# Last stage of a hybrid encoder block: the gated embedding is added to the residual by adding transfers, its squares are queued further back, and two column pairs take another order of units

## The chip, the cores and the metric

The kernel runs on one core of a Trainium2 chip. The metric is the device time of one execution in microseconds (us); the kernel before took 2026.38 us in the median of three runs (2024.7 to 2027.43).

## The reference

One layer on 256 rows of width 4096 in float32: an input product of 4096 by 14336, attention heads beside a convolution module, an output product that gives the residual `h`, and then the last stage, where the change lies:

```python
gate = jax.nn.sigmoid(rms_norm(h, ple_norm_g[i]) @ w_ple_gate[i] + b_ple_gate[i])
h = h + gate * (p[i] @ w_ple[i])
...
return rms_norm(h, final_g)
```

`w_ple_gate` is 4096 by 4096, `p[i]` is 256 by 256 and `w_ple` 256 by 4096.

## The kernel before, in words

**Products.** Every weight is split into a high part `wh` (a cast on ScalarE, ACT in the profile, L204) and a low part `wl` (weight minus high part, on VectorE, DVE, L205), and so is every operand. A product is then three matmuls of 128 by 512: high by high, low by high, high by low. Weights come in tiles `wt` of 128 rows by 1024 columns: two column blocks of 512 side by side. There are five buffers for `wt`, three each for `wh` and `wl`, two each for the sums `u`, `uh` and `ul` (the pools of L73 and L1085).

**Units.** `mixed_product` (L377) computes one pair of column blocks for both halves of the rows, in 16 units of two row blocks of weights each. A plain unit makes eight products (24 matmuls). A unit marked with a star in the order makes seven (21 matmuls), after Strassen: DVE builds the sums `ua` and `ub` of weight tiles (L518, L519, L531, L532), ACT and DVE split them as they split weights, and some products go to four helper banks (P1, P5, P6, P7) in place of the four accumulators. Its operands on the other side are combinations of row blocks made beforehand (`hS`, or the spare places that `combine_into_places`, L370, fills for pair 13). A minus in the order lets a transfer that adds, issued on GpSimd's queue (POOL), make the low part of the second weight tile: ACT writes the cast and its negative `low` (L215, L217), and the transfer adds the weight to `low`.

**Orders.** The stars stand in tables of numbers. `dense` has eight starred units, `denser` has nine, three of its units with a minus:

```python
dense = units("1 0* 3 2* 5 4* 6* 7 8* 9 10* 11 12* 14* 13 15")
denser = units("1 0* 3 2* 5 4* 13* 7- 6*- 8* 10*- 9 12* 14* 11 15")
```

**The last stage.** There are eight column blocks, so four pairs, `c0` = 0, 2, 4 and 6. The first three are made by `gated_pair` (L1236), with the orders `late`, `dense`, `dense`; the fourth has its own code from L1280 on with the order `final`. After its 16 units a pair makes the embedding `p @ w_ple` by `product` (L243), 24 matmuls into the banks `ps_tmp` that the helpers also use: there are four, and the embedding holds all of them until DVE has multiplied each by its gate. The gate of a quarter (row half h, column block j) is made by L1266 and a sigmoid on ACT (L1267). What then follows waits in the list `later`, of which `fill` takes four entries at the end of each unit of the next pair: the multiply of gate and embedding into `gt` (a half of a tile `z`), the add of `gt` to the residual `hc`, the sum of squares of `hc` (on ACT, L610) and the multiply of `hc` by the final weights (`fgs`). Entries of `later` all run under L184.

**What sets the order.** Each engine runs its instructions in one fixed order. The program's order is the wish; a scheduler fixes the queue of each engine when the kernel is built, and may move an instruction forward past others. The bias rows `rows` and the final weights `fgs` share three buffers with the rows that combinations are made in, so a load of one waits on its queue (SP) until another is done with.

Of the kernel before, what the change touches and what calls it, by code (L numbers as in the profile page):

```python
# [13 lines left out]
ALU = mybir.AluOpType  # L14
# [3 lines left out]
NB = 512  # L18
# [7 lines left out]
def hybrid_block(  # L26
# [23 lines left out]
    nc = tc.nc  # L50
# [129 lines left out]
    later = deque()  # L180
# [62 lines left out]
    def product(w, col, lhs, kblocks, pool=None, tag="acc", fills=2):  # L243

        acc = [
            (pool or ps_acc).tile([P, NB], F32, tag=tag, name=f"acc{h}") for h in range(NH)
        ]
        for k0 in range(0, kblocks, KC):
            kc = min(KC, kblocks - k0)
            wh, wl = weight_parts(w, col, k0, kc)  # L250
            for k in range(kc):
                for h in range(NH):
                    accumulate(acc[h], h, lhs, k0 + k, wh, wl, k, kblocks)
            fill(fills)
        return acc
# [10 lines left out]
    def sum_rows():  # L266
        return [spool.tile([P, NB], F32, tag="row", name="comb", bufs=3) for _ in range(2)]
# [33 lines left out]
    def combine_again(dst, at, t, i, rows, then=lambda ins: None, at_places=None):  # L301

        a, s = rows
        then(
            nc.vector.tensor_tensor(
                a.rearrange("q (i t) -> q i t", t=T), t[:, i : i + 2, 0, :].bitcast(F32),
                t[:, i : i + 2, 1, :].bitcast(F32), ALU.add,
            )
        )
        return combined_parts(  # L310
            dst, at, s, a[:, :T], a[:, T : T + P], a[:, T + P :], 1.0, then, at_places
        )
# [27 lines left out]
    def units(text):  # L340

        return [
            (int(u.rstrip("*+-")), "".join(f for f in "*+" if f in u), "-" in u)
            for u in text.split()
        ]


    dense = units("1 0* 3 2* 5 4* 6* 7 8* 9 10* 11 12* 14* 13 15")
    denser = units("1 0* 3 2* 5 4* 13* 7- 6*- 8* 10*- 9 12* 14* 11 15")
# [12 lines left out]
    late = units("1 3 5 7 9 11 13 15 0* 2 4* 6 8* 10* 12 14")  # L362

    def spare_places(tiles):

        return [[t[:, 0, q, P:] for q in range(2)] for t in tiles]
# [3 lines left out]
    def combine_into_places(pair, tiles):  # L370

        rows = sum_rows()
        places[pair] = spare_places(tiles[:4])
        t, i = tiles[pair // 2], pair % 2 * 2
        combine_again(None, None, t, i, rows, at_places=places[pair])()

    def mixed_product(  # L377
# [93 lines left out]
        for n, (pair, seven, by_dma) in enumerate(order):  # L471
# [82 lines left out]
            if begins and on_begin:  # L554
                on_begin()
# [13 lines left out]
    tt, stt = nc.vector.tensor_tensor, nc.vector.scalar_tensor_tensor  # L569
    QUARTERS = ((0, 0), (1, 0), (0, 1), (1, 1))  # L570

    def helper_sums(helper, z):


        nc.scalar.copy(z[1][0], helper["P1"])
        tt(z[1][0], helper["P6"], z[1][0], ALU.add)
        tt(z[0][1], helper["P5"], z[1][0], ALU.add)
        tt(z[1][0], helper["P7"], z[1][0], ALU.add)
        tt(z[1][1], helper["P5"], z[1][0], ALU.add)

    def sum_tiles(*homes):

        homes = homes or (dict(tag="stage"),) * 2
        t = [spool.tile([P, NH, NB], F32, name="z", **kw) for kw in homes]
        return t, [[t[j][:, h] for j in range(2)] for h in range(NH)]
# [57 lines left out]
    def first_pairs(add):  # L643
# [62 lines left out]
        for n in range(1, n_x + 1):  # L706
# [26 lines left out]
    rows = [(conv_ln_g, KCW), (conv_ln_b, KCW), (b_dw, KCW), (attn_out_g, AW // P),  # L733
            (conv_out_g, KCW), (ple_norm_g, KD)]
# [332 lines left out]
    def broadcast_row(src, n0, n, **kw):  # L1067

        kw = kw or dict(tag="row", bufs=3)
        t = spool.tile([P, n], F32, name="row", **kw)  # L1070
        nc.sync.dma_start(
            t, bass.AP(tensor=src.tensor, offset=src.offset + n0, ap=[[0, P], [1, n]])
        )
        return t
# [13 lines left out]
    for c0, order in zip(range(0, CW // NB, 2), point):  # L1088
        row = broadcast_row(b_pw, c0 * NB, 2 * NB, tag="stage")
        rows = [row[:, j * NB : (j + 1) * NB] for j in range(2)]  # L1090
# [85 lines left out]
    hs, hT, hS = [], [], []  # L1176
# [20 lines left out]
    for c0 in range(0, D // NB, 2):  # L1197
        for j in range(2):
            hc = act.tile([P, NH, NB], F32, tag="act", name="hc")
            c = c0 + j  # L1200
# [19 lines left out]
        for h, j in QUARTERS:  # L1220
            hc = hs[c0 + j][:, h, :]
# [10 lines left out]
    ssq_f = cpool.tile([P, NH, n_f + 2], F32, name="ssq_f")  # L1232
    nc.vector.memset(ssq_f[:, :, :1], EPS)
    square_f = partial(square_sum, scale=D ** -0.5)

    def gated_pair(c0, order, ahead):  # L1236

        z, rows, fgs = [], [], []

        def on_begin():  # L1240
            rows.extend(broadcast_row(b_ple_gate, (c0 + j) * NB, NB) for j in range(2))

        def on_helpers(helper):
            z.extend(sum_tiles()[1])
            stt(z[0][0], helper["P1"], r_h[:, :1], rows[0], ALU.mult, ALU.add)
            helper_sums(helper, z)
            for h, j in QUARTERS[1:]:
                zz = z[h][j]
                stt(
                    zz, zz, r_h[:, h : h + 1], rows[j],  # L1250
                    ALU.mult, ALU.subtract if j else ALU.add,
                )
            fgs.extend(broadcast_row(final_g, (c0 + j) * NB, NB) for j in range(2))

        acc = mixed_product(
            w_ple_gate[0], c0 * NB, hT, hS, order, on_helpers, ahead=ahead, fills=(4,),
            on_begin=on_begin,
        )
        pacc = [
            product(w_ple[0], (c0 + j) * NB, pT, PLE // P, pool=ps_tmp, tag="tmp", fills=0)  # L1260
            for j in range(2)
        ]
        todo = []
        for h, j in QUARTERS:
            gt, hc = z[h][j], hs[c0 + j][:, h, :]
            stt(gt, acc[h][j], r_h[:, h : h + 1], gt, ALU.mult, ALU.subtract if j else ALU.add)  # L1266
            nc.scalar.activation(gt, gt, AF.Sigmoid)  # L1267
            later.append(partial(tt, gt, pacc[j][h], gt, ALU.mult))
            todo.append(partial(tt, hc, hc, gt, ALU.add))
            todo.append(partial(square_f, ssq_f[:, h, 1 + c0 + j : 2 + c0 + j], hc))  # L1270
            todo.append(partial(tt, hc, hc, fgs[j], ALU.mult))
        later.extend(todo)

    for c0 in range(0, n_f - 2, 2):
        gated_pair(c0, dense if c0 else late, None if c0 else h_ahead)


    c0 = n_f - 2
# [9 lines left out]
    rows, fgs = [], []  # L1288

    def on_begin():  # L1290
        rows.extend(broadcast_row(b_ple_gate, (c0 + j) * NB, NB) for j in range(2))

    def scaled(h, j):
        zz = z[h][j]
# [2 lines left out]
    def on_helpers(helper):  # L1297
# [3 lines left out]

    acc, add_left = mixed_product(
        w_ple_gate[0], c0 * NB, hT, hS, final, on_helpers, fills=(4,), on_begin=on_begin,
        left=[None] * 3 + [kept] * 3,
    )
# [73 lines left out]
    squares = []  # L1379
# [45 lines left out]
```

## Time and profile before

| | |
|---|---|
| median of three runs | 2026.38 us |
| the profiled execution's own time | 2025.85 us |
| span of its profile | 2024.1 us |
| granted clock of TensorE over the span | 0.998 |
| `c0` = 2, from 1739.57 to 1826.60 us | 87.03 us |
| `c0` = 4, from 1826.60 to 1914.50 us | 87.90 us |

A stretch here goes from the start of the last matmuls of one pair (where L1266 begins) to the same place of the next. PE is TensorE's matmuls, PEld its weight loads, SP the queue that issues most transfers. The busy time of an engine counts overlapping instructions once; the mean duration of a DVE instruction is some 0.08 us longer than the distance to the next when they stand back to back.

### The profile page before, as it was taken

The numbers are of one execution on the slowest core, as the hardware profiler recorded it, in microseconds if no ns is written. First come the engines' busy times: TensorE is split into PE (matmuls) and PEld (weight loads), VectorE is DVE, ScalarE is ACT, GpSimd is POOL, SyncE is SP. The second block draws the span as 40 slices with busy tenths as digits, with TensorE's granted clock in tenths as the row PEclk, the third lists the DMA queues.
The fourth block names the chain that finished last, engine by engine and source line by source line (L and its number), as shares of the span: only waits on it lengthen the run. The fifth ranks groups of instructions, "written<-read, shape, count | busy, mean of one in ns | idle before, by whom it ended". The sixth has DMA issues, their size and how long they took to land.

```text
span 2024.1 us, 26329 instructions
## 1 busy us (share of the span) xinstructions
PE 2006.7 (99%) x9043; PEld 1648.0 (81%) x9043; DVE 1926.9 (95%) x2771; ACT 1257.1 (62%) x1634; POOL 65.3 (3%) x71
## 2 busy tenths in 40 slices
PE   9999999999999999999999999999999999999997
PEld 7888888878888888788888888887888888888876
DVE  7999999899999999888999999999999999999998
ACT  7655555665666556776566676765766766656565
POOL 0000000000000000000000000000000000000000
PEclk9999999999999999999999999999999999999999
DMA  8788878679668877556677786876767766666765
GB/s 290 225 233 241 249 221 250 178 220 257 200 198 257 255 206 235 164 176 205 202 239 215 225 244 209 240 239 204 236 215 230 234 200 200 211 218 206 232 207 180
DMA packets 174193, 447.72 MB, mean 221 GB/s; under 512 B 14302, under 2 KB 17518, under 8 KB 174058
## 3 DMA queue, kind: packets, MB, share of 16 engines
q1 hardware_dynamic: 161952, 417.93, 63.8%
q0 software_dynamic: 11456, 27.27, 7.9%
q8 instruction: 71, 1.16, 0.2%
q10 hardware_dynamic: 650, 0.84, 0.1%
q14 instruction: 64, 0.52, 0.1%
HBM read 441.78 MB, written 4.19 MB: 220 GB/s over the span
## 4 chain that ended last, share of the span: by engine, by line
PE 89%; DVE 6%; issue 2%; DMA 1%; ACT 1%; POOLq 0%; POOL 0%; ACTq 0%; DVEq 0%; SPq 0%
PE acc L420 68%; PE acc_P L420 17%; DVE wl L205 2%; DMA wt<-in_w_in_dram 1%; PE tmp_ps L170 1%; DVE cv L787 1%; PE acc L237 1%; DVE ul L205 1%; PE tmp_ps L959 0%; PE tmp_ps L943 0%; PE tmp_ps L977 0%; ACT uh L204 0%; DVE cv L868 0%; ACT wh L204 0%; PE tmp_ps L982 0%
## 5 line engine op out<-in xcount | busy, mean ns | idle before, releaser
L420 PE MATMUL acc<-wh,big_t 128*128 128x512 f32 x4028 | 1240.3, 391 | 0.9 <-ACT big_t L156 0.4
L204 ACT CAST wh<-wt 128x1024 fp32r<-128x1024 f32 (+1 forms) x716 | 684.3, 965 | 493.8 <-PE acc L420 351.7
L420 PEld LDWEIGHTS acc<-wh,big_t 128*128 128x128 f32 x4028 | 753.3, 188 | 157.1 <-issue 1.3
L205 DVE TENSOR_TENSOR wl<-wt,wh 128x1024 fp32r<-128x1024 f32 (+1 forms) x716 | 788.8, 1113 | 33.0 <-ACT wh L204 27.5
L420 PE MATMUL acc<-wl,big_t 128*128 128x512 f32 x1958 | 756.4, 392 | 0.3 <-DVE wl L205 0.2
L420 PEld LDWEIGHTS acc<-wl,big_t 128*128 128x128 f32 x1958 | 367.2, 188 | 78.1 <-DVE wl L205 2.7
L204 ACT CAST uh<-ua 128x1024 fp32r<-128x1024 f32 x187 | 196.6, 1051 | 103.0 <-DVE ua L519 51.7
L205 DVE TENSOR_TENSOR ul<-ua,uh 128x1024 fp32r<-128x1024 f32 x187 | 228.1, 1220 | 6.9 <-ACT uh L204 4.2
L787 DVE SCALAR_TENSOR_TENSOR cv<-uT,dw,cv 128x255 f32<-128x255 f32 (+23 forms) x480 | 203.6, 463 | 1.1
L420 PE MATMUL acc_P<-uh,big_t 128*128 128x512 f32 x570 | 174.6, 391 | 0.1
L204 ACT CAST uh<-ub 128x1024 fp32r<-128x1024 f32 x99 | 104.2, 1053 | 47.9 <-DVE ub L532 39.2
L420 PEld LDWEIGHTS acc_P<-uh,big_t 128*128 128x128 f32 x570 | 106.0, 188 | 24.5 <-ACT uh L204 3.3
L205 DVE TENSOR_TENSOR ul<-ub,uh 128x1024 fp32r<-128x1024 f32 x99 | 120.8, 1220 | 0.8 <-ACT uh L204 0.5
L420 PE MATMUL acc_P<-ul,big_t 128*128 128x512 f32 x285 | 109.7, 392 | 0.2 <-DVE ul L205 0.2
L420 PE MATMUL acc<-uh,big_t 128*128 128x512 f32 x286 | 88.6, 390 | 0.0
L420 PE MATMUL acc_P<-wh,big_t 128*128 128x512 f32 x286 | 88.3, 389 | 0.0
L518 DVE TENSOR_TENSOR ua<-wt 128x512 f32<-128x512 f32 x112 | 76.9, 686 | 10.0 <-DMA wt<-in_w_in_dram 6.2
L519 DVE TENSOR_TENSOR ua<-wt 128x512 f32<-128x512 f32 x112 | 76.8, 686 | 2.7 <-DMA wt<-in_w_in_dram 1.7
L420 PE MATMUL acc_P<-uh,comb_t 128*128 128x512 f32 x228 | 70.3, 391 | 0.3 <-ACT uh L204 0.2
L532 DVE TENSOR_TENSOR ub<-ub,wt 128x512 f32<-128x512 f32 x99 | 68.1, 688 | 1.4
L531 DVE TENSOR_TENSOR ub<-ua,wt 128x512 f32<-128x512 f32 x99 | 67.8, 685 | 0.0
L420 PEld LDWEIGHTS acc_P<-ul,big_t 128*128 128x128 f32 x285 | 53.3, 188 | 13.9 <-DVE ul L205 3.0
(254 smaller groups left out, 1631.0 us busy)
## 6 DMA issues: line engine op xcount, KB each, us to landing
wt<-in_w_in_dram SPq DMA_DIRECT2D x416, 512.0 KB, 4.7
wt<-in_w_out_dram SPq DMA_DIRECT2D x128, 512.0 KB, 4.5
wt<-in_w_ple_gate_dram SPq DMA_DIRECT2D x128, 512.0 KB, 4.2
wt<-in_w_pw_dram SPq DMA_DIRECT2D x32, 512.0 KB, 4.9
ua<-in_w_in_dram SPq DMA_DIRECT2D x31, 512.0 KB, 4.3
ua<-in_w_in_dram POOLq DMA_DIRECT2D x31, 512.0 KB, 8.8
wt<-in_w_in_dram SPq DMA_DIRECT2D x31, 256.0 KB, 2.8
low<-in_w_in_dram POOLq DMA_DIRECT2D x12, 512.0 KB, 8.2
```

The costliest lines, as they stand in the source:

```text
L170: nc.tensor.transpose(pt[:, i * T + h * P : i * T + (h + 1) * P], src[:, h, b] if len(src.shape) == 4 else src[:, h, b * P : (b + 1) * P], ...
L204: nc.scalar.copy(wh[:, :kc, :], wt[:, :kc, :]),
L205: nc.vector.tensor_tensor(wl[:, :kc, :], wt[:, :kc, :], wh[:, :kc, :].bitcast(F32), ALU.subtract),
L237: nc.tensor.matmul(acc, a, b[:, k, :], start=kb == 0 and kind == 0, stop=kb == kblocks - 1 and kind == 2,)
L420: nc.tensor.matmul(banks[name], a, b, start=name not in begun, stop=final and ends[name] == n and kind == 2 and not (left and name in "P2 ...
L518: plus(ua[:, 0], w0[:, 0], w0[:, 1])
L519: plus(ua[:, 1], w0[:, 1], w1[:, 1])
L531: plus(ub[:, 0], ua[:, 0], w1[:, 1])
L532: plus(ub[:, 1], ub[:, 0], w1[:, 0])
L787: nc.vector.scalar_tensor_tensor(cv[:, i, PAD - k :], uT[:, i, : T + k - PAD], dw[:, b, k : k + 1], cv[:, i, PAD - k :], ALU.mult, ALU.add,)
```

## The change

Three things change, all in the last stage.

1. The add of `gt` to `hc` becomes an adding transfer on POOL's queue, asked for right behind its multiply. The squares and the multiplies by the final weights go behind eight empty entries in `later`, so at the earliest two units later by the program's order.
2. The bias rows are no longer asked for as soon as the first starred unit has begun, but through `later`, behind the entries that are there already (the final weights' multiplies of the pair before).
3. Pairs `c0` = 2 and 4 take the order `denser` instead of `dense`, and behind `c0` = 0 stands `combine_into_places(13, hT)`, which makes the operands that unit 13 needs for its star.

```diff
+    def bias_row(rows, c):
+        rows.append(broadcast_row(b_ple_gate, c * NB, NB))
+
     def gated_pair(c0, order, ahead):
...
         def on_begin():
-            rows.extend(broadcast_row(b_ple_gate, (c0 + j) * NB, NB) for j in range(2))
+            later.extend(partial(bias_row, rows, c0 + j) for j in range(2))
...
-        todo = []
+        squares, weights = [], []
         for h, j in QUARTERS:
...
             later.append(partial(tt, gt, pacc[j][h], gt, ALU.mult))
-            todo.append(partial(tt, hc, hc, gt, ALU.add))
-            todo.append(partial(square_f, ssq_f[:, h, 1 + c0 + j : 2 + c0 + j], hc))
-            todo.append(partial(tt, hc, hc, fgs[j], ALU.mult))
-        later.extend(todo)
+            later.append(partial(nc.gpsimd.dma_start, hc, gt, accum_op=ALU.add))
+            squares.append(partial(square_f, ssq_f[:, h, 1 + c0 + j : 2 + c0 + j], hc))
+            weights.append(partial(tt, hc, hc, fgs[j], ALU.mult))
+        later.extend([lambda: None] * 8 + squares + weights)
 
     for c0 in range(0, n_f - 2, 2):
-        gated_pair(c0, dense if c0 else late, None if c0 else h_ahead)
+        gated_pair(c0, denser if c0 else late, None if c0 else h_ahead)
+        if c0 == 0:
+            combine_into_places(13, hT)
```

The fourth pair's `on_begin` changes like the first.

The change moves instructions at each of the three borders between pairs. Two queues are shown at the first of them, where the first units of `c0` = 2 begin. On ACT before, behind the cast `uh` of the first starred unit's sum, the casts of the weights go on; the first square stands behind the cast of `ub`:

```order
L204 CAST uh_15712<-ua_15709 128x1024 [waits DVE_49]
L204 CAST wh_15716<-wt_15699 128x1024 [waits DMAHW4_49,PE_49,Activation_49]
L204 CAST wh_15761<-wt_15757 128x1024 [waits DMAHW5_49,DVE_49,PE_49]
L204 CAST wh_15777<-wt_15759 128x1024 [waits DMAHW6_49,DVE_49,PE_49]
L204 CAST uh_15723<-ub_15720 128x1024 [waits DVE_49]
L610 ACTIVATE junk_15753,ssq_f_14773<-hc_11728 128x512
L204 CAST wh_15803<-wt_15799 128x512 [waits DMAHW7_49,PE_49,Activation_49]
L610 ACTIVATE junk_15793,ssq_f_14773<-hc_11728 128x512 [waits DVE_49,Activation_49]
```

On ACT now (DMASW is a transfer of POOL's queue):

```order
L204 CAST uh_15727<-ua_15724 128x1024 [waits DVE_49]
L610 ACTIVATE junk_15886,ssq_f_14773<-hc_11728 128x512 [waits DMASW4_49]
L610 ACTIVATE junk_15888,ssq_f_14773<-hc_11728 128x512 [waits DMASW5_49,Activation_49]
L204 CAST wh_15731<-wt_15714 128x1024 [waits DMAHW3_49,PE_49]
L204 CAST uh_15738<-ub_15735 128x1024 [waits DVE_49]
L204 CAST wh_15771<-wt_15767 128x1024 [waits DMAHW4_49,PE_49]
L204 CAST wh_15787<-wt_15769 128x1024 [waits DMAHW5_49,PE_49]
L610 ACTIVATE junk_15890,ssq_f_14773<-hc_11730 128x512 [waits DMASW6_49,Activation_49]
L204 CAST wh_15807<-wt_15803 128x512 [waits DMAHW6_49,DVE_49,PE_49]
L610 ACTIVATE junk_15892,ssq_f_14773<-hc_11730 128x512 [waits DMASW7_49,Activation_49]
```

The scheduler has moved the first two squares forward, into the first starred unit: they stand ahead of the cast of that unit's second weight tile, and each waits for its adding transfer.

On DVE before, at the same place, all four multiplies of gate and embedding (`z` from `acc0` or `acc1`) stand ahead of the low part of that second tile (`wl_15717`), and the first two adds behind it:

```order
L184 TENSOR_TENSOR z_15518<-acc0_15605,z_15518 128x512 [waits PE_49,Activation_49]
L184 TENSOR_TENSOR z_15518<-acc1_15606,z_15518 128x512 [waits PE_49,Activation_49]
L519 TENSOR_TENSOR ua_15709<-wt_15697,wt_15699 128x512 [waits DMAHW4_49]
L184 TENSOR_TENSOR z_15519<-acc0_15625,z_15519 128x512 [waits PE_49,Activation_49]
L205 TENSOR_TENSOR wl_15678<-wt_15659,wh_15677 128x1024 [waits DMAHW0_49,DVE_49,Activation_49]
L184 TENSOR_TENSOR z_15519<-acc1_15626,z_15519 128x512 [waits PE_49]
L205 TENSOR_TENSOR wl_15706<-wt_15697,wh_15705 128x512 [waits DVE_49,Activation_49]
L205 TENSOR_TENSOR ul_15713<-ua_15709,uh_15712 128x1024 [waits Activation_49]
L205 TENSOR_TENSOR wl_15717<-wt_15699,wh_15716 128x1024 [waits PE_49,Activation_49]
L531 TENSOR_TENSOR ub_15720<-ua_15709,wt_15699 128x512
L184 TENSOR_TENSOR hc_11728<-hc_11728,z_15518 128x512
```

On DVE now (the same unit's second tile is `wt_15714`):

```order
L184 TENSOR_TENSOR z_15518<-acc0_15605,z_15518 128x512 [waits PE_49,Activation_49]
L184 TENSOR_TENSOR z_15518<-acc1_15606,z_15518 128x512 [waits PE_49,Activation_49]
L519 TENSOR_TENSOR ua_15724<-wt_15712,wt_15714 128x512 [waits DMAHW3_49]
L531 TENSOR_TENSOR ub_15735<-ua_15724,wt_15714 128x512 [waits DVE_49]
L205 TENSOR_TENSOR wl_15693<-wt_15674,wh_15692 128x1024 [waits DMAHW0_49,Activation_49]
L205 TENSOR_TENSOR wl_15721<-wt_15712,wh_15720 128x512 [waits DVE_49,PE_49,Activation_49]
L205 TENSOR_TENSOR ul_15728<-ua_15724,uh_15727 128x1024 [waits Activation_49]
L532 TENSOR_TENSOR ub_15735<-ub_15735,wt_15714 128x512 [waits DVE_49]
L205 TENSOR_TENSOR wl_15732<-wt_15714,wh_15731 128x1024 [waits PE_49,Activation_49]
L184 TENSOR_TENSOR z_15519<-acc0_15625,z_15519 128x512
L205 TENSOR_TENSOR ul_15739<-ub_15735,uh_15738 128x1024 [waits Activation_49]
L184 TENSOR_TENSOR z_15519<-acc1_15626,z_15519 128x512
```

The four adds are gone from DVE, and the last two multiplies have moved behind the low part of the second tile.

More of the change, by code (lines that the diff above doesn't have):

```diff
@@ L1290, in on_begin @@
     def on_begin():
-        rows.extend(broadcast_row(b_ple_gate, (c0 + j) * NB, NB) for j in range(2))
+        later.extend(partial(bias_row, rows, c0 + j) for j in range(2))
     def scaled(h, j):
```

## The prediction

> **What bounds the kernel now.** I read the page first, then the windows of the last stage, then who waits there, and last the timelines at a border between two pairs.
>
> ```profile
> PE 2006.7 (99%) x9043; PEld 1648.0 (81%) x9043; DVE 1926.9 (95%) x2771; ACT 1257.1 (62%) x1634; POOL 65.3 (3%) x71
> ```
> ```profile
> 1739.57:1826.60 87.03, 86.98 (x383) 70.95 (x382) 86.37 (x107) 53.51 (x64) 0.00 (x0) 1.00 0.66 212
> 1826.60:1914.50 87.90, 87.90 (x386) 71.69 (x385) 87.11 (x107) 52.20 (x63) 0.00 (x0) 1.00 0.68 215
> 1914.50:1987.50 73.00, 72.92 (x315) 57.78 (x314) 72.03 (x89) 44.22 (x55) 0.00 (x0) 1.00 0.66 208
> ```
>
> The columns of the windows are length, then busy time and count of PE, PEld, DVE, ACT and POOL, granted clock, DMA share. The rows are the pairs `c0` = 2, 4 and most of 6. PE is never idle, but DVE is busy 86.37 of 87.03, 87.11 of 87.90 and 72.03 of 73.00 us. Two engines bound the stage together: time taken from PE alone brings little, and what DVE loses is soon felt. That it is felt already, the waits of the third window show; the chain of waits gives PE's pace.
>
> ```profile
> ACT wh L204 <- PE acc L420: 20.5, 11, 3.5
> ...
> PEld acc_P L420 <- ACT uh L204: 2.5, 9, 0.5
> ```
> In the second window the same wait is shorter:
> ```profile
> PEld acc_P L420 <- ACT uh L204: 1.0, 4, 0.3
> ```
> ```profile
> 1728.57 11.56 PE acc L420 x51
> ```
>
> 11.56 us for 51 matmuls are 0.227 each. ACT has room (it waits 20.5 us for PE to give buffers back), yet PE waits for casts of sums, which ACT can only make when DVE has made the sums.
>
> **Edit 3, the order of units.** Up to unit 10 a pair had five plain and six starred units; now it has four and seven. One plain unit less and one starred more saves PE three matmuls, 0.68 us per pair, 1.36 in all. DVE's prices are distances between starts in this timeline of DVE at the first border:
>
> ```profile
> 1737.83 0.69 DVE L518 TENSOR_TENSOR ua<-wt 128x512 f32<-128x512 f32 x1 [1.01 <-DMA wt<-in_w_ple_gate_dram]
> ...
> 1743.34 1.28 DVE L184 TENSOR_TENSOR z<-acc,z 128x512 f32<-128x512 f32 x2
> ...
> 1748.07 1.22 DVE L205 TENSOR_TENSOR ul<-ua,uh 128x1024 fp32r<-128x1024 f32 x1
> 1749.23 1.23 DVE L205 TENSOR_TENSOR wl<-wt,wh 128x1024 fp32r<-128x1024 f32 x1
> 1750.38 0.69 DVE L531 TENSOR_TENSOR ub<-ua,wt 128x512 f32<-128x512 f32 x1
> 1750.98 0.68 DVE L184 TENSOR_TENSOR hc<-hc,z 128x512 f32<-128x512 f32 x1
> 1751.58 0.69 DVE L532 TENSOR_TENSOR ub<-ub,wt 128x512 f32<-128x512 f32 x1
> ```
>
> A full tile is 1.15 (1749.23 to 1750.38), a half 0.60. A starred unit costs 3 x 1.15 + 5 x 0.60 = 6.4, a plain one 2.3, and each minus takes 1.15 off: 6.4 - 2.3 - 3.4 = +0.7 us for DVE up to unit 10. Since DVE sets the pace there, the saved matmuls vanish under it. `combine_into_places` adds one half-tile sum and eight small instructions, once:
>
> ```profile
> L305 DVE TENSOR_TENSOR comb<-big_t 128x512 f32<-128x512 f32 x18 | 12.4, 686 | 0.1
> ...
> L184 DVE TENSOR_TENSOR hc<-hc,z 128x512 f32<-128x512 f32 x12 | 8.1, 685 | 0.0
> ...
> L286 DVE TENSOR_TENSOR big_t<-comb,big_t 128x128 fp32r<-128x128 f32 x8 | 2.1, 284 | 0.0
> ```
>
> The sum falls ahead of the border, where DVE stood idle for 1.01 us (row of 1737.83); eight times 0.284 less the overlap of 0.08 make +1.6 us in `c0` = 2.
>
> **Edit 1, the adds.** Four adds less at each of three borders: 4 x 0.60 = 2.4 us of DVE, the change's gain. In their place stand twelve transfers, whose landing the squares wait for. No row shows a small adding transfer from on-chip memory; the nearest:
>
> ```profile
> wt<-in_w_ple_gate_dram SPq DMA_DIRECT2D x128, 512.0 KB, 4.2
> ua<-in_w_in_dram POOLq DMA_DIRECT2D x31, 512.0 KB, 8.8
> ...
> low<-in_w_in_dram POOLq DMA_DIRECT2D x12, 512.0 KB, 8.2
> ...
> out_dram<-hc SPq DMA_DIRECT2D x12, 256.0 KB, 2.4
> ```
> ```profile
> DMA to landing us min/median/max: 5.8/8.3/10.0
> ```
> ```profile
> 1526.61 0.87 POOL L524 DMA_DIRECT2D low<-in_w_out_dram  x1 [5.65 <-PE acc_P L420]
> ```
>
> The lower bound is 2.4 us (a plain transfer of the same tile), the upper 8.2 (an adding one of twice the size). A plain transfer of half the size takes 2.4 / 4.2 = 0.57 of the time; 0.57 x 8.2 = 4.7. I take 4.5, as the last stage's DMA share is low (0.66). Two adds, issued 0.87 apart on POOL, carry what one `low` carries: I take 6.5 from the first issue to the second landing, near the shortest `low` (5.8). The Trainium skill (DMA: Bandwidth & Descriptors, section "Anatomy of one DMA — SWDGE (gpsimd) path") gives such a transfer about 2.0 us plus its bytes at 436 GB/s, which would be 2.6 us here; for 512 KB it gives 3.2, and the rows above say 8.2, so I do not take it.
>
> Now the first border, with ACT and PE before:
>
> ```profile
> 1745.95 1.05 ACT L204 CAST uh<-ua 128x1024 fp32r<-128x1024 f32 x1
> 1748.15 1.06 ACT L204 CAST wh<-wt 128x1024 fp32r<-128x1024 f32 x1 [1.14 <-issue]
> ...
> 1753.68 0.63 ACT L610 ACTIVATE junk<-hc 128x512 bf16<-128x512 f32 x1
> ...
> 1754.30 0.61 ACT L204 CAST wh<-wt 128x512 fp32r<-128x512 f32 x1
> ```
> ```profile
> 1752.21 0.61 PE L420 MATMUL acc_P<-uh,big_t 128*128 128x512 f32 x2
> ```
>
> - The first multiply ends at 1744.0, POOL issues at 1744.1, the two adds land at 1748.6 and 1750.6.
> - ACT reaches the first square at 1747.0, stands still, squares until 1751.2 (0.62 each), and casts the second weight tile until 1752.25, where it was done at 1749.2.
> - DVE now has two multiplies less (1.2) and one sum more (0.6) ahead of `ul`, so it is ready for that tile's low part at 1749.2, and waits 3.1 us. Behind it stands the multiply of the third quarter, which frees a helper's bank: PE wants it at 1752.21 and gets it at 1754.1.
> - That multiply sends the third add only at 1754.1, so it lands at 1758.6. The third square stands ahead of the cast for unit 3, which is done at 1758.6 + 0.62 + 0.61 = 1759.8; DVE, ready at 1758.2 after three full tiles and a multiply, waits 1.6 us more.
>
> DVE loses 4.7, saves 2.4, and pays 1.6 and 0.7 for edit 3: **+4.6 us** in `c0` = 2.
>
> At the other borders the schedule is milder: all four multiplies stand ahead of the blocked cast.
>
> ```profile
> 1829.65 1.22 DVE L205 TENSOR_TENSOR wl<-wt,wh 128x1024 fp32r<-128x1024 f32 x1
> ...
> 1832.68 1.88 DVE L184 TENSOR_TENSOR z<-acc,z 128x512 f32<-128x512 f32 x3
> ...
> 1841.02 1.22 DVE L205 TENSOR_TENSOR wl<-wt,wh 128x1024 fp32r<-128x1024 f32 x1
> ```
> ```profile
> 1830.45 1.05 ACT L204 CAST wh<-wt 128x1024 fp32r<-128x1024 f32 x1
> ...
> 1835.85 1.06 ACT L204 CAST wh<-wt 128x1024 fp32r<-128x1024 f32 x1 [2.05 <-PE acc L420]
> 1836.81 1.05 ACT L204 CAST uh<-ua 128x1024 fp32r<-128x1024 f32 x1
> 1838.61 2.00 ACT L204 CAST wh<-wt 128x1024 fp32r<-128x1024 f32 x2 [0.76 <-ACT uh L204]
> ```
>
> At the second, the first multiply is over at 1833.3, so the second add lands at 1839.9; the casts follow from 1840.5 instead of 1838.6, and DVE waits 0.6 and 0.8 us, then 0.6 behind the fourth square. Its own row has worsened by 1.3 us: a low part that stood between the multiplies now stands ahead of them all and waits for its cast (from 1830.8 to 1831.5, 0.7), and the next full tile, which DVE reaches at 1836.3, waits for the cast of 1835.85, which waits for a buffer (0.6). 2.0 + 1.3 - 2.4 + 0.7 = **+1.6 us**. The third border has the second square further back: 1.9 + 1.3 - 2.4 = **+0.8 us**, with no new order.
>
> **Edit 2, the bias rows.**
>
> ```profile
> row<-in_b_ple_gate_dram SPq DMA_DIRECT2D x8, 256.0 KB, 4.7
> ```
>
> They are used at a pair's last starred unit, asked for now around unit 8, five units ahead (25 us, where a row lands in 4.7): nothing. If the buffer they wait for is late, the second weight tile of unit 8 stands behind them on SP; its cover is two units, some 10 us. Bounds: 0 and +2 us per pair.
>
> **Sum.** +4.6 + 1.6 + 0.8 = +7.0 us. On the profiled execution's 2025.85 that is 2032.9; the median lies 0.5 above, so I forecast 2033.4.
>
> **Rivals.**
> 1. *The adds land in time.* If an add takes 2.4 us and the pair 3.3, the squares find their data at all borders: -2.4 + 1.6 + 0.7, -2.4 + 1.3 + 0.7 and -2.4 + 1.3, so -1.6 us, 2024.8. For it: the plain row of 2.4. Against it: no `low` lands in under 5.8. It decides where an add lands in under some 3 us. The formula of the Trainium skill quoted above would make this the result.
> 2. *The gain shows in full*, faster than before: with rival 1, and without the 1.3 us of worse rows and the small waits, PE's waits go (2.5 us in the fourth pair, 1.0 in the third) and the six matmuls count: -1.4 - 3.5 = -4.9 us, 2021.5. It decides where adds land under 3 us and casts stay ahead. Against it: DVE's rows as they now stand.
> 3. *Adding transfers keep their price at half the size*: 8.2 us for one, 9.1 for two. The second landing is 2.6 us later at each border, and at the first the third add costs 3.6 more on top: +6.2, +2.6 and +2.6 on +7.0, so +18.4, 2044.8. For it: if most of 8.2 were a fixed cost; against it: the shortest `low` is 5.8. POOL's row, 0.87 us beside a DVE that is busy 98%, shows no delay at the issue. The Trainium skill (SBUF — State Buffer, section "SBUF: two separate sides") warns that descriptors made on GpSimd can starve while DVE holds a port that both share; by it this rival would be likelier.
> 4. *The bias rows hold up SP* in two pairs, on top of my sum: +3, 2036.5.
>
> **How the numbers follow.** Forecast 0.60, rival 1 0.16, rival 2 0.07, rival 3 0.11, rival 4 0.06. One microsecond of landing moves the sum by 4 to 5 us, so the forecast's own case (4 to 5.2 us for one) spans 2030 to 2038. Leaving out rival 2 and the far end of rival 3, the range is 2024.5 to 2043. A measurement of this kernel tells 0.2% (4 us) from no change: faster (below 2022.3) 0.06, same 0.24 (rival 1 and the low end of the forecast), slower 0.70.
>
> **What would show it.** Right: ACT idle ahead of squares (L610), released by the adding transfers, twice in `c0` = 2; DVE idle ahead of `wl` by ACT, 4 to 5 us there and about 2 at each later border; PE stopped in the first starred unit of each pair; `hc<-z` on POOL landing in 4 to 6 us; `c0` = 2 some 5 us longer. Wrong: adds landing under 3.5 us, squares without idle time before them, and pairs of 86 to 87 us.

## The result, and the profile after

The changed kernel took 2038.13 us in the median of six runs (2036.36 to 2041.15), the kernel before 2026.24 in six beside them: slower by 0.6%, a ratio of 1.006 (95% interval 1.0047 to 1.0073), where 2033.4 was forecast. The profiled execution took 2038.09 us; its span is 2036.3 us against 2024.1 before.

The windows of the changed kernel, by the same marks as before (length, then busy time of PE, PEld, DVE, ACT and POOL, granted clock):

```profile
1739.12:1834.30 95.18, 89.93 (x380) 71.18 (x379) 85.89 (x113) 58.26 (x73) 6.19 (x7) 0.98 0.75 220
1834.30:1926.40 92.10, 89.53 (x383) 72.19 (x382) 85.97 (x106) 56.49 (x68) 6.14 (x7) 0.98 0.79 234
1926.40:1999.40 73.00, 72.57 (x315) 57.99 (x314) 70.61 (x86) 44.24 (x55) 3.54 (x4) 1.00 0.75 229
```

Pair `c0` = 2 takes 95.18 us instead of 87.03, `c0` = 4 takes 92.10 instead of 87.90: +8.2 and +4.2. From there to the end of the span it is 109.9 instead of 109.6 us, and the stage's first mark comes 0.45 us earlier; the sum is +12.2, the difference of the spans. PE, which was idle for 0.05 us at most in either pair, now stands: it is busy for 89.93 of 95.18 us and for 89.53 of 92.10. DVE is less busy than before in both pairs.

The waits of the changed kernel from 1735 us to 2000 (total, times, longest):

```profile
ACT junk L610 <- DMA hc<-z: 16.3, 10, 3.8
DVE wl L205 <- ACT wh L204: 12.0, 8, 3.5
...
PEld acc_P L420 <- ACT uh L204: 8.0, 15, 2.9
```

Before, no square waited for a transfer, and DVE's wait was this:

```profile
DVE wl L205 <- ACT wh L204: 1.1, 3, 0.5
```

The waits of the changed kernel are a chain: the squares wait for the adding transfers, DVE waits for the casts behind the squares, and PE waits for what both of them make of the sums. At the first border, ACT:

```profile
1748.28 0.63 ACT L610 ACTIVATE junk<-hc 128x512 bf16<-128x512 f32 x1 [1.74 <-DMA hc<-z]
...
1750.62 0.63 ACT L610 ACTIVATE junk<-hc 128x512 bf16<-128x512 f32 x1 [1.62 <-DMA hc<-z]
...
1751.25 1.03 ACT L204 CAST wh<-wt 128x1024 fp32r<-128x1024 f32 x1
...
1758.93 0.63 ACT L610 ACTIVATE junk<-hc 128x512 bf16<-128x512 f32 x1 [3.80 <-DMA hc<-z]
...
1762.63 0.63 ACT L610 ACTIVATE junk<-hc 128x512 bf16<-128x512 f32 x1 [2.47 <-DMA hc<-z]
```

DVE there:

```profile
1752.32 1.23 DVE L205 TENSOR_TENSOR wl<-wt,wh 128x1024 fp32r<-128x1024 f32 x1 [3.47 <-ACT wh L204]
1753.46 0.68 DVE L184 TENSOR_TENSOR z<-acc,z 128x512 f32<-128x512 f32 x1
...
1760.19 0.69 DVE L205 TENSOR_TENSOR wl<-wt,wh 128x512 fp32r<-128x512 f32 x1 [2.05 <-ACT wh L204]
1764.33 1.23 DVE L205 TENSOR_TENSOR ul<-ua,uh 128x1024 fp32r<-128x1024 f32 x1 [1.03 <-ACT uh L204]
```

And PE:

```profile
1754.20 0.73 PE L420 MATMUL acc_P<-uh,big_t 128*128 128x512 f32 x2 [2.30 <-DVE z L184]
...
1770.82 0.79 PE L420 MATMUL acc_P<-ul,big_t 128*128 128x512 f32 x1 [1.66 <-DVE ul L205]
```

Read them by time: two squares hold the cast `wh` back to 1751.25, DVE stands for 3.47 us until it is made, the multiply behind (1753.46) frees PE's helper bank late, and PE stands. Then the third and the fourth square do the same to later casts, and the delay reaches PE again, most of all at 1770.82. At the second border PE has one stop of this kind:

```profile
1852.23 0.89 PE L420 MATMUL acc_P<-uh,big_t 128*128 128x512 f32 x2 [2.52 <-ACT uh L204]
```

One thing more stands in these windows: a granted clock of 0.98. Shorter windows show what it is an average of:

```profile
1770.73:1774.15 3.42, 3.33 (x8) 2.65 (x9) 3.42 (x5) 0.06 (x1) 0.00 (x0) 0.50 0.74 224
1774.15:1777.57 3.42, 3.42 (x17) 2.79 (x16) 2.09 (x6) 1.47 (x2) 0.00 (x0) 1.00 0.63 234
1852.65:1856.07 3.42, 3.42 (x10) 2.68 (x9) 3.42 (x5) 1.46 (x5) 0.00 (x0) 0.50 0.80 201
```

Behind the stops of 1770.82 and 1852.23 the clock is 0.50 for 3.4 us, once in each of the two pairs. Half of 3.42 us of matmuls is lost (8 begin where 17 do in the next stretch), some 1.7 us each time.

### The profile page after: what moved, and what is told of

Read it like the earlier page. It is cut to its first block, busy times and chain, and to the rows that moved or that the text cites. A ratio compares the mean times of both kernels' runs of the same rounds, so it can differ in the third digit from the quotient of the medians.

```text
span 2036.3 us, 26372 instructions
## 1 busy us (share of the span) xinstructions
PE 2010.6 (99%) x9037; PEld 1649.2 (81%) x9037; DVE 1924.6 (95%) x2774; ACT 1265.9 (62%) x1648; POOL 81.2 (4%) x89
## 5 line engine op out<-in xcount | busy, mean ns | idle before, releaser
L204 ACT CAST wh<-wt 128x1024 fp32r<-128x1024 f32 (+1 forms) x710 | 676.8, 963 | 471.3 <-PE acc L420 338.6
L420 PE MATMUL acc<-wl,big_t 128*128 128x512 f32 x1930 | 747.4, 392 | 0.1
L420 PEld LDWEIGHTS acc<-wl,big_t 128*128 128x128 f32 x1930 | 362.4, 188 | 75.8 <-DVE wl L205 0.9
L787 DVE SCALAR_TENSOR_TENSOR cv<-uT,dw,cv 128x255 f32<-128x255 f32 (+23 forms) x480 | 208.6, 485 | 1.1
L420 PE MATMUL acc_P<-uh,big_t 128*128 128x512 f32 x582 | 179.1, 392 | 5.8 <-ACT uh L204 3.5
```

What stands on the lines that cost most here:

```text
L204: nc.scalar.copy(wh[:, :kc, :], wt[:, :kc, :]),
L420: nc.tensor.matmul(banks[name], a, b, start=name not in begun, stop=final and ends[name] == n and kind == 2 and not (left and name in "P2 ...
L787: nc.vector.scalar_tensor_tensor(cv[:, i, PAD - k :], uT[:, i, : T + k - PAD], dw[:, b, k : k + 1], cv[:, i, PAD - k :], ALU.mult, ALU.add,)
```

## The experiments

Three theories stood at the start. Theory 1: the cost is the place of the squares on ACT, ahead of casts, where they wait for transfers. Theory 2: it is the denser order of units, which asks more of DVE. Theory 3: it is the adding transfers as such, by what they load. Ratios are to the kernel before, timed beside each, with their 95% intervals. Differences between runs that were timed in different groups are good to about 1 us, since the median of the kernel before itself lay between 2025.21 and 2026.24 in them.

Edit 2 needs no run: with the bias rows asked for early again, the changed kernel has the same instructions in the same order, with the same waits, on all five queues.

### e1: squares that wait for no transfer

```diff
-            squares.append(partial(square_f, ssq_f[:, h, 1 + c0 + j : 2 + c0 + j], hc))
+            squares.append(partial(square_f, ssq_f[:, h, 1 + c0 + j : 2 + c0 + j], gt))
```

> The changed kernel, but the squares of the first three pairs read the gated embedding (a tile that a multiply on VectorE makes) instead of the residual, so they wait for no adding transfer; the adding transfers, the multiplies and the order of units stay. It leaves out the sum of squares of the residual of those pairs (another sum stands in its place). Theory 1 (squares on ScalarE stand ahead of the casts and wait for the adding transfers): all of the 11.9 us that the change cost goes, and some of the 2.4 us per border that VectorE saves comes out: 2020 to 2027 us, no granted clock of 0.5 inside the last stage, TensorE's stalls at the first two borders under 3 us each (8.9 and 5.3 in the changed kernel). Theory 2 (the denser order of units and the operands made for it): 2035 to 2039 us. Theory 3 (the adding transfers as such, by what they load): 2035 to 2039 us.

Measured: 2026.66 us, ratio 0.9997 (0.9988 to 1.0006). The loss is gone. Two squares still stand ahead of the second tile's cast at the first border (they begin at 1743.69 and 1745.77, the cast at 1746.44), but now neither waits. The windows of the stage's first two pairs:

```profile
1735.00:1835.00 100.00, 99.24 (x433) 80.16 (x432) 97.35 (x128) 65.64 (x85) 7.95 (x9) 1.00 0.81 242
1835.00:1927.00 92.00, 91.94 (x403) 74.40 (x402) 89.74 (x111) 60.19 (x72) 6.14 (x7) 1.00 0.83 246
```

PE is full again, and the clock is 1.00. The twelve transfers are still there, and no quicker; the last number is the median time from issue to landing, first in the changed kernel, then here:

```profile
hc<-z POOLq DMA_DIRECT2D x12, 256.0 KB, 5.1
```
```profile
hc<-z POOLq DMA_DIRECT2D x12, 256.0 KB, 5.5
```

So theory 3 falls: the transfers cost nothing that can be measured while no square waits for them. Theory 2 falls as the cause of this loss. Of a gain over the kernel before, which theory 1's range of 2020 to 2027 left room for, nothing shows.

### e2: squares behind the casts

```diff
+    def held(dst, src):
+        with queued_behind(list(recent)):
+            square_f(dst, src)
...
-            squares.append(partial(square_f, ssq_f[:, h, 1 + c0 + j : 2 + c0 + j], hc))
+            squares.append(partial(held, ssq_f[:, h, 1 + c0 + j : 2 + c0 + j], hc))
```

> The changed kernel, but each square of the first three pairs may not be queued ahead of the cast that was made last where the program asks for the square. It stands some six casts later on ScalarE and still waits for its adding transfer. Theory 1 (the squares' place on ScalarE): the transfers have landed when the squares come up, so 2020 to 2028 us. Theory 2 (the denser order): 2035 to 2039 us. Theory 3 (the adding transfers as such): 2035 to 2039 us.

Measured: 2025.49 us, ratio 0.9999 (0.9990 to 1.0007). The first and the fourth of ACT's squares; none of the four has idle time ahead of it:

```profile
1761.31 0.62 ACT L610 ACTIVATE junk<-hc 128x512 bf16<-128x512 f32 x1
...
1763.95 0.63 ACT L610 ACTIVATE junk<-hc 128x512 bf16<-128x512 f32 x1
```

The first stands at 1761.31 instead of 1748.28. This is the window of the first border and its pair, and the landings of the twelve transfers:

```profile
1735.00:1835.00 100.00, 98.33 (x432) 80.30 (x431) 97.22 (x127) 64.89 (x81) 7.90 (x9) 1.00 0.80 241
```
```profile
DMA to landing us min/median/max: 4.2/6.1/8.4
```

PE is busy for 98.33 of 100 us at full clock, beside transfers that land no sooner: the wish to run the squares later is met only now. Theory 1 holds, and the change without that place shows neither gain nor loss.

### e3: the adds on DVE

```diff
-            later.append(partial(nc.gpsimd.dma_start, hc, gt, accum_op=ALU.add))
+            later.append(partial(tt, hc, hc, gt, ALU.add))
```

> The changed kernel, but the residual's adds are done by VectorE, as before, in place of the adding transfers; the rest of the change stays. Theory 1 (the wait for transfers on ScalarE): that wait goes, VectorE has 2.4 us more at each border: 2025 to 2031 us. Theory 2 (the denser order): 2035 to 2040 us. Theory 3 (the adding transfers as such): 2025 to 2031 us too, so this run tells theory 2 from the other two, and the other runs tell theory 1 from theory 3.

Measured: 2036.9 us, ratio 1.0045 (1.0031 to 1.0060). Theory 1's number missed: with no transfer to wait for, the time is nearly the same, in theory 2's range. The squares did not stop waiting, though. They now wait for DVE's adds:

```profile
ACT junk L610 <- DVE hc L184: 7.3, 5, 2.0
```

PE feels it little at the first border, where it is busy for 29.00 of 29.00 us from 1735 to 1764. The loss is elsewhere. Here are windows of this kernel well behind that border, and PE's stops in them:

```profile
1764.00:1781.00 17.00, 16.86 (x74) 13.19 (x72) 17.00 (x29) 10.51 (x15) 0.00 (x0) 1.00 0.64 215
1781.00:1802.00 21.00, 17.12 (x73) 13.57 (x74) 20.93 (x27) 14.48 (x17) 2.67 (x3) 0.99 0.91 255
```
```profile
1782.23 0.73 PE L420 MATMUL acc<-wl,big_t 128*128 128x512 f32 x2 [1.38 <-DVE wl L205]
1801.12 1.00 PE L420 MATMUL acc<-low,big_t 128*128 128x512 f32 x2 [2.65 <-DMA low<-in_w_ple_gate_dram]
```

DVE is busy 17.00 of 17.00 and 20.93 of 21.00 us. It falls behind in the middle of the pair, where the denser order asks most of it. The first stop waits for DVE, the second for a transfer that makes a low part; behind that one too the clock is halved, from 1801.41 to 1804.82. That is theory 2's place, with a loss of its own that the changed kernel does not have. That the adds make the difference is argued from DVE's load here; e6 tests the order alone.

### e4: the order of before

```diff
-        gated_pair(c0, denser if c0 else late, None if c0 else h_ahead)
-        if c0 == 0:
-            combine_into_places(13, hT)
+        gated_pair(c0, dense if c0 else late, None if c0 else h_ahead)
```

> The changed kernel with the order of units of before for the second and third pair, and without the operands made for unit 13's star; adding transfers and late squares stay. Theory 1 (squares on ScalarE): the waits stay, so most of the loss stays: 2033 to 2040 us. Theory 2 (the denser order and what VectorE has to make for it): 2023 to 2028 us. Theory 3 (the adding transfers as such): 2033 to 2040 us.

Measured: 2046.9 us, ratio 1.0103 (1.0089 to 1.0118). Theory 2 falls by sign: without the denser order the loss is larger, past theory 1's range (2033 to 2040) too. Its waits:

```profile
ACT junk L610 <- DMA hc<-z: 29.5, 12, 4.5
...
PEld acc_P L420 <- DVE z L184: 7.5, 3, 2.9
```

Twelve squares of twelve wait, 29.5 us instead of 16.3. PE stands at every border for a multiply that frees its bank, where the changed kernel does so once (1754.20), and three halved stretches follow its stops instead of two.

### e5 and e6: the two sides of the order

e5 is e2 and e4 together. e6 is the kernel before with the order alone:

```diff
-        gated_pair(c0, dense if c0 else late, None if c0 else h_ahead)
+        gated_pair(c0, denser if c0 else late, None if c0 else h_ahead)
+        if c0 == 0:
+            combine_into_places(13, hT)
```

> The changed kernel with the squares held behind the casts and, beside that, the order of units of before (no unit 13 with a star, no operands made for it). What is left of the change: adding transfers, squares held. Theory 1 (all that the change lost is the squares' place on ScalarE, 20.8 us of it under this order): 2024 to 2028 us; TensorE had only some 3 us of stalls in this stage before, so 7 us less work on VectorE can give no more than that. Rival (adding transfers do not go with this order, since no unit takes its low part by a transfer and VectorE makes them all): 2035 to 2047 us.

> The kernel before with one part of the change alone: the denser order for the second and third pair and the operands made for unit 13; adds on VectorE, squares and bias rows as before. Theory 2b (VectorE was full already, and the denser order asks 0.7 us more of it per pair and 1.6 us once, in a stretch in which TensorE saves 0.7 us): it falls behind in the middle of the pairs as where the adds were put back on it (2036.9 us): 2030 to 2037 us. Rival (that run lost its 11 us by the place of the late squares, which waited on ScalarE for VectorE's adds): 2024 to 2027 us.

Measured: e5 2025.27 us, ratio 0.9998 (0.9989 to 1.0007); e6 2031.05, ratio 1.0028 (1.0017 to 1.0038). The ranges of both theories hold, and their rivals fall. In the windows of e5 PE has no room:

```profile
1735.00:1835.00 100.00, 99.74 (x440) 82.06 (x439) 96.10 (x117) 61.15 (x74) 4.42 (x5) 1.00 0.73 227
1835.00:1927.00 92.00, 92.00 (x406) 75.68 (x405) 90.11 (x109) 56.55 (x67) 4.34 (x5) 1.00 0.76 231
```

Twelve adds less on DVE bring nothing that can be measured, since PE was busy all the time before. In e6 PE's weight loads wait little and often for sums, and PE's matmuls stand four times, for 0.44 to 1.08 us, where no stop of 0.2 us or more stood before. The weight loads' waits from 1735 to 2000 us, first in the kernel before, then in e6:

```profile
PEld acc_P L420 <- ACT uh L204: 4.1, 15, 0.5
```
```profile
PEld acc_P L420 <- ACT uh L204: 10.8, 25, 1.5
```

So the denser order costs 5.6 us where DVE does the adds (e6) and nothing that can be measured where transfers do them and the squares stand behind the casts (e2 beside e5). It looks as if the adds' saving pays for the order, but e2 and e6 differ in the place of the squares and of the final weights' multiplies too, so that is argued and not shown. The order's six matmuls less would bring 1.4 us if PE alone counted; e2's trace has a stop of that size, for a low part that lands late:

```profile
1794.53 0.50 PE L420 MATMUL acc<-low,big_t 128*128 128x512 f32 x1 [1.36 <-DMA low<-in_w_ple_gate_dram]
```

What e3 loses beyond e6, some 5 to 6 us, goes with what else e3 changes, the later place of the squares and of the final weights' multiplies with the adds on DVE; that was not taken apart further.

### e7 and e9: one border at a time

e7 holds the squares at the first border alone, e9 at the other two:

```diff
+            squares.append(partial(square_f if c0 else held, ssq_f[:, h, 1 + c0 + j : 2 + c0 + j], hc))
```
```diff
+            squares.append(partial(held if c0 else square_f, ssq_f[:, h, 1 + c0 + j : 2 + c0 + j], hc))
```

> The changed kernel with the squares held behind the casts at the first border alone; at the other two they stand as in the change. Theory 1 (each border's loss is its own squares' wait, with the clock halved behind it): the first border's share goes, 7 to 9 us: 2029 to 2032 us, with TensorE's stall of 2.7 us at the second border still there. Rival (the loss only moves to the next border, or is one of the order): 2034 to 2039 us.

> The changed kernel with the squares held behind the casts at the second and third border; at the first they stand as in the change, two of them ahead of the casts of the first starred unit. Theory 1 (the loss is that of the squares ahead of the casts, border by border): the loss of the first border alone is left, TensorE's stalls of 6 us there and 1 to 2 us of halved clock: 2031 to 2035 us. Rival (the loss moves to another border when it is taken from one): 2035 to 2040 us.

Measured: e7 2034.8 us, ratio 1.0048 (1.0036 to 1.0061), a miss for theory 1's numbers and inside the rival's; e9 2032.26, ratio 1.0032 (1.0020 to 1.0045), as theory 1 has it. In e7 the stop of the first border is gone, but the third has a new one:

```profile
1937.43 1.22 PE L420 MATMUL acc_P<-uh,big_t 128*128 128x512 f32 x2 [3.62 <-ACT uh L204]
```

The order of ACT's queue tells why. At the third border, the changed kernel has one square ahead of the cast `uh<-ub`, which PE waits for:

```
L204 CAST uh<-ua 128x1024 [waits DVE_49]
L610 ACTIVATE junk,ssq_f<-hc 128x512 [waits DMASW2_49]
L204 CAST wh<-wt 128x1024 [waits DMAHW1_49,PE_49,Activation_49]
L204 CAST wh<-wt 128x1024 [waits DMAHW2_49,PE_49,Activation_49]
L204 CAST uh<-ub 128x1024 [waits DVE_49]
```

In e7 the scheduler put two there:

```
L204 CAST uh<-ua 128x1024 [waits DVE_49]
L610 ACTIVATE junk,ssq_f<-hc 128x512 [waits DMASW2_49]
L610 ACTIVATE junk,ssq_f<-hc 128x512 [waits DMASW3_49,Activation_49]
L204 CAST wh<-wt 128x1024 [waits DMAHW1_49,PE_49]
L204 CAST wh<-wt 128x1024 [waits DMAHW2_49,PE_49]
L204 CAST uh<-ub 128x1024 [waits DVE_49]
```

So it is the same mechanism at a border that had been spared, not a loss of the order. The first border by itself costs 2032.26 - 2025.49 = 6.8 us (e9 less e2), or 7.6 when each is first compared with the kernel before timed beside it. Its two halved stretches in e9:

```profile
1754.91:1758.32 3.41, 3.38 (x8) 2.71 (x9) 3.41 (x4) 0.96 (x2) 1.73 (x2) 0.50 0.87 219
1771.98:1775.39 3.41, 3.41 (x10) 2.65 (x9) 3.41 (x5) 0.00 (x0) 0.00 (x0) 0.50 0.81 261
```

### e10: one square ahead instead of two

```diff
+            squares.append(partial(held if squares else square_f, ssq_f[:, h, 1 + c0 + j : 2 + c0 + j], hc))
```

> The changed kernel with one square in place of two ahead of the casts at every border (the first of each pair stands where the change puts it, the other three are held). Theory 1 with its slack (ScalarE can wait for one transfer before TensorE runs out; two are too many, as the third border of the changed kernel, which has one ahead, lost under 1 us): 2025 to 2029 us. Rival (any wait for a transfer ahead of the casts costs its border): 2031 to 2036 us.

Measured: 2028.14 us, ratio 1.0013 (1.0005 to 1.0022), theory 1's range; three borders together cost 2.6 us more than e2 (3.5 when each is first compared with the kernel before beside it). The first border of e10, ACT and then PE:

```profile
1749.25 0.63 ACT L610 ACTIVATE junk<-hc 128x512 bf16<-128x512 f32 x1 [1.51 <-DMA hc<-z]
```
```profile
1766.82 0.50 PE L420 MATMUL acc_P<-ul,big_t 128*128 128x512 f32 x1 [1.00 <-DVE ul L205]
```

ACT waits 1.51 us for the first transfer, nearly as long as in the changed kernel, and PE's stop at 1754 is gone. The casts had slack for most of one wait, not for the second.

### e8: the freed time spent on more starred units

e2 with unit 11 starred too in the second and third pair, unit 13 in the last, and more low parts by transfers:

```diff
+    densest = units("1 0* 3 2* 5 4* 13* 7- 6*- 8* 9- 10*- 11*- 12* 14* 15")
-    final = units("1 0* 3 2* 5 4* 6* 7 8* 9 10* 12* 11 13 14 15")
+    final = units("1 0* 3 2* 5 4* 6*- 7 8* 9 10*- 13* 12* 11 14 15")
...
+            combine_into_places(
+                11, hT, spare_places(hT[4:7]) + [[hT[6][:, 2, q, P:] for q in range(2)]]
+            )
```

> The changed kernel with the squares held behind the casts, and the work that VectorE no longer has spent on more starred units: unit 11 as well in the second and third pair (its operands are made into spare places like those of unit 13), unit 13 in the last pair, and more low parts by adding transfers. TensorE has 15 matmuls less than in the kernel before, 3.4 us. If TensorE alone sets the stage once no wait stands on ScalarE: 2021 to 2024 us. If VectorE is full or the transfers for the low parts come too late: 2026 to 2036 us.

Measured: 2036.64 us, ratio 1.0059 (1.0046 to 1.0071). This try for a faster kernel failed, with a time just past the range given for a full VectorE or late transfers. It has 3.4 us of matmuls less in all, and PE stands for 2.6, 3.1 and 5.1 us in its three windows:

```profile
1735.00:1835.00 100.00, 97.40 (x425) 79.23 (x424) 97.68 (x135) 69.72 (x89) 7.92 (x9) 1.00 0.81 242
1835.00:1927.00 92.00, 88.86 (x384) 70.85 (x384) 89.02 (x111) 61.20 (x73) 7.91 (x9) 1.00 0.84 248
1927.00:2000.00 73.00, 67.93 (x285) 53.16 (x284) 68.50 (x84) 45.13 (x55) 5.27 (x6) 0.98 0.78 234
```

Which part of it is DVE's load and which the six low parts more on POOL's queue was not taken apart. No version measured here beats the kernel before by more than the measurement can tell.

## Why the prediction was right, and where its sizes were off

**Direction and mechanism: right.** The squares stand ahead of the casts and wait for transfers; e1, e2 and e10 show it by taking away the data, the place, and one of the two squares.

**The first border's times: right, up to a point.** Landings at 1748.6 and 1750.6 were forecast, the squares began at 1748.28 and 1750.62; the cast over at 1752.25, it was at 1752.28; DVE's wait 3.1, it was 3.47; the bank at 1754.1, it was 1754.20; the third landing 1758.6, its square at 1758.93. The price of an adding transfer, worked out from rows of other tiles (4.5 us for one), was the sum's most uncertain term, and the twelve took 4.1 to 7.1 us:

```profile
DMA to landing us min/median/max: 4.1/5.1/7.1
```

The Trainium skill (DMA: Bandwidth & Descriptors, section "Anatomy of one DMA — SWDGE (gpsimd) path") would give 2.6 us as an estimate from its figures. The shortest here took 4.1, so by the trace that is too low for this kind of transfer.

**What the +4.6 lacked.** It stopped at the third square. The fourth waited 2.47 us more, ahead of the cast `uh` that DVE then waited 1.03 for, and the waits before it were 0.37 and 0.45 longer: DVE lost 6.55 instead of 4.7. And the halved clock, 1.7 us, was in no term. 4.6 + 1.85 + 1.7 = 8.15, where the pair lost 8.15. The -2.4, +1.6 and +0.7 that stand in the 4.6 did no harm there, since they all but cancel.

**The other borders: partly luck.** At the second, +1.6 was forecast and +4.2 measured, about what PE's stop of 2.52 and the clock's 1.7 make together. At the third, +0.8 was forecast and +0.3 measured, but as the difference of two errors: DVE's waits of 3.2 us and a gain of 2.4. DVE did wait for ACT in that pair, 2.2 us in all (0.8 before), but PE stood for 0.37 us only:

```profile
1942.11 1.23 DVE L205 TENSOR_TENSOR ul<-ub,uh 128x1024 fp32r<-128x1024 f32 x1 [1.41 <-ACT uh L204]
```
```profile
1942.13 0.73 PE L420 MATMUL acc_P<-uh,big_t 128*128 128x512 f32 x2 [0.37 <-ACT uh L204]
```

**The step that failed: "4 x 0.60 = 2.4 us of DVE, the change's gain".** I set what DVE saves against what it waits, as if one engine's account were the stage's. PE had no idle time to win back (87.90 of 87.90 us busy), so time saved on DVE cannot come out, while time in which PE stands is lost for good. The 2.5 and 1.0 us that I read as PE's waits were those of its weight loads, beside matmuls that were busy for 72.92 of 73.00 us and for 87.90 of 87.90. e5 measures the gain: 2025.27 beside 2025.41, nothing in place of 7.2. The other side of the same step: the denser order was charged 1.6 + 0.7 + 0.7 = 3.0 us, and costs nothing that shows with the adds off DVE (e2) and 5.6 with them on it (e6). The two terms together were forecast at -7.2 + 3.0 = -4.2 us; e2's median is 0.6 below that of the kernel before, and its interval holds no change. The waits, 4.7 + 3.3 + 3.2 = 11.2 in the forecast, cost 2038.13 - 2025.49 = 12.6 with the halved clock in it (e2 has all of the change but the squares' place). So of the 4.9 us that the forecast of +7.0 was short, about 3.6 are a gain that could not show and about 1.4 are waits and clock. That those two totals came so close is luck too: the clock's 3.4 us were missing, and the third border's 3.2 were nearly all too much.

**Bias rows: nothing, as forecast,** and more simply than I argued: the edit moves no instruction, so the rival that had them hold up SP falls with it.

**Rivals.** The adds didn't land in time where the squares stood, and did where e2 put them, without a gain. The full gain of 4.9 us is refuted by e2 and e5. A price of 8.2 us for one adding transfer is refuted by the landings. The warning that descriptors made on GpSimd can starve while DVE holds the port that they share (Trainium skill, SBUF — State Buffer, section "SBUF: two separate sides") does not show as a cost: e2's transfers land in 4.2 to 8.4 us beside a DVE busy for 97.22 of 100 us, and its time is that of before. No row shows whether DVE held that port.

## What to carry to other kernels

An entry of a list that is taken up "two units later" is not yet two units later on its engine: read the queue that the scheduler makes, and ask of each wait on a transfer what stands behind it there. Where one engine is busy without a gap, take work from another only to spend it, and count its saving as nothing until the full engine has less to do; a stop of the full engine is lost whole. A cast that has slack for a wait for one transfer may not have it for two, so move the smallest number of instructions.

## What the runs showed of the hardware that was not expected

**Short stops halve the clock, by where they fall on a grid of 3.413 us.** Before, the stage ran at a granted clock of 1.00 from 1739.57 to 1987.50. In the changed kernel, e3, e4, e8 and e9 stretches of 3.41 us at 0.50 follow stops of PE, and in e7 one of twice that, behind the 3.62 us of 1937.43:

```profile
1936.44:1943.27 6.83, 5.84 (x14) 4.58 (x15) 5.68 (x8) 2.81 (x6) 0.00 (x0) 0.50 0.69 191
```

The length of a stop does not decide by itself. Of two stops with the same order of instructions, 2.30 us at 1754.20 in the changed kernel was not followed by a halved stretch, and this one in e9 was (the stretch of 1754.91, above):

```profile
1754.94 1.22 PE L420 MATMUL acc_P<-uh,big_t 128*128 128x512 f32 x2 [2.32 <-DVE z L184]
```

The starts of the halved stretches tell why. They lie 1852.65 - 1770.73 = 81.92 us apart in the changed kernel and 1771.98 - 1754.91 = 17.07 in e9, which is 24 and 5 times 3.413; every other trace with two or more agrees. So divide a trace into windows of 3.413 us from such a start, backwards too. The stop of 2.30 us lies across a boundary, 1.76 us ahead of it and 0.54 behind; that of 2.32 lies in one window but for 0.03. The windows that hold three stops of the changed kernel, and then the one of e9 (length, then PE's busy time):

```profile
1750.25:1753.66 3.41, 1.65 (x8) 1.03 (x6) 1.34 (x2) 3.04 (x5) 0.00 (x0) 1.00 0.59 215
1767.32:1770.73 3.41, 1.59 (x6) 0.67 (x4) 3.41 (x5) 3.41 (x4) 0.00 (x0) 1.00 0.57 161
1849.24:1852.65 3.41, 0.89 (x5) 0.43 (x4) 1.66 (x2) 3.41 (x6) 1.00 (x2) 1.00 1.02 238
```
```profile
1751.50:1754.91 3.41, 1.12 (x5) 0.58 (x4) 1.85 (x3) 3.41 (x6) 0.00 (x0) 1.00 0.39 156
```

Behind the first the clock stays 1.00; behind the other three it is 0.50 for the next window. The same holds in all twelve traces from 100 to 2000 us: eleven windows at full clock have PE busy for 0.77 to 1.60 us, and each is followed by one at 0.50; in all others PE is busy for 1.65 us or more, and none is. So stops that fall into one window add up: that of 1770.82 (1.66 us) came with 0.25 us more in its window, while in e4 a stop of 1.66 us alone in its window (1771.85) was followed by no halved stretch. The Trainium skill (TensorE: Matmul & The Clock Gate, Part 1) has the half rate come after an idle window of some 3.4 us; the length of the stretches agrees, but here a window with PE busy for up to 1.60 us of it was enough.

**An adding transfer of half the size took more than half the time.** 256 KB between tiles took 5.1 us in the median, 512 KB from the weights 7.8 (`low`, same stage, changed kernel): two thirds of the time for half the bytes. The source differs too, so the size alone is not shown to do it:

```profile
low<-in_w_ple_gate_dram POOLq DMA_DIRECT2D x6, 512.0 KB, 7.8
```
